# A two-layer decoder trunk: PSUM tiles of two banks, weight blocks split by alternate rows, and seven products in three column groups of a chunk's first block

## Chip, cores and metric

The kernel runs on one core of one Trainium2 chip. The metric is device time in microseconds (us) of one execution, lower is better. Three runs of the kernel before took 2023.47, 2025.87 and 2023.33 us, with a median of 2023.47.

## What is computed

The reference is a trunk of two layers over 256 tokens of width 2048, in float32. Layer 0 mixes by trailing means over windows of 2, 4, 8 and 16 tokens, layer 1 by causal dilated attention with 16 heads of 128; each mixer is followed by a layer norm with a scaled residual, a gated feed-forward block with a causal convolution of width 3, and another layer norm.

```python
# layer 0                                     # layer 1
mix = pool_mixer(h, w_in, w_grp, scale, w_out) # or dilated_attention(h, k, v, w_q, w_o)
h = layer_norm(ALPHA * h + mix, ln1_g, ln1_b)
u = h @ w_up                                   # 2048 -> 2 * 5504
c = conv_b + sum(conv_w[j] * shifted(u, j))    # width 3, causal
gate, val = split(c)
h = layer_norm(ALPHA * h + (silu(gate) * val) @ w_down, ln2_g, ln2_b)
```

Some 380 MB of weights are read once, and nearly all the arithmetic is matrix products of 256 tokens with those weights.

## The kernel before

**Products in two parts.** Each float32 operand is split into a high part, which the reduced float32 format of TensorE holds, and a low part, the rest. `do_split` (L74) makes the two parts of a weight block of 512 rows by 512 columns: ScalarE copies the high part `wh` (L82), VectorE subtracts to get the low part `wl` (L83). A product is then high times high, high times low and low times high.

**Units.** The work is a list `units`; each entry is one weight block, what TensorE does with it, and what follows once the group is closed (`post`). `run_units` (L126) goes through the list in order. Ahead of unit i it issues loads of up to 5 later units (three `raw` buffers, SyncE's queue) and splits of up to 3 later units (four buffers of `wh` and `wl`). Then TensorE's instructions of the unit are issued, then whatever `later(n, fn)` put off until now, then the unit's `post`. All engines work in this program order.

**Two kinds of group.** `group` (L177) with `mm_quad` (L150) makes features by tokens: four PSUM banks (`acc`, one per 128 output features), filled over several units, with one matmul of 512 columns (`wh` on both parts of the activations, L165) and one of 256 (`wl` on the high part, L166) for each 128 by 128 block. The last unit of a group goes bank by bank, the others row block by row block. `group_tm` (L189) makes tokens by features for the down projection and for V: banks `t0`, `t1`, and a unit either takes the plain way, 24 matmuls of 512 columns (`go_t`, L232, L238 to L240), or the way of seven products.

**Seven products.** For a block listed in `sevens`, the 512 by 512 weight block and the activations are cut in two by two parts, and seven products of sums of parts replace eight. Sums of weights are made by `split_sums` (L90) in two units, "a" and "b", out of one raw block; sums of activations by `left_sums` (L623), which takes the fourth of them, `own`, either at once or, through `own_at`, later with `last` (L661), where the plain way still needs the place in the tile `g` that it is written to. The unit pair has 42 matmuls of 256 columns (L227 to L229) into four banks, `t0`, `t1`, `s2`, `s3`. `early_post` (L822) folds the two `s` banks into the token tile `ht`, by accumulating DMAs on GpSimd's queue or by VectorE; `tm_post` (L844) adds the `t` banks.

**Feed-forward order.** Blocks of 512 hidden features are called q = 0 to 10. The down projection is made in chunks of blocks: 0 to 2, 3 to 5, 6 and 7, 8 to 10. Within a chunk there are four column groups c = 0 to 3 of 512 output columns. `weave` (L713) puts the units of chunk 0 and chunk 1 between units of the next up projections: four up units and three down blocks to one c. Blocks q = 0 and q = 3, the first of their chunks, take seven products in c = 2 and c = 3 only; the others of these chunks take them in every c.

**PSUM.** The pool `psp` holds eight tiles of one bank, handed out in program order (`bank`). Evacuation goes bank by bank: ScalarE copies one half, VectorE adds the other (L577 and L578 for up projections, L1020 and L1021 for Q and K, L473 and L475 for the mixer), or VectorE adds both halves onto the residual (L320 and L322 in `resid_last`, L313).

**Layer norm at the end of a layer.** `add_last` (L458) runs four groups c = 0 to 3 of the last projection onto the residual H[0] to H[3]. After c = 0, `shift` (L362) takes an estimate `cs` of the token means; it is subtracted from H[0] by VectorE (L372). For layer 0's feed-forward block, where `shifted` is set, it is taken off the other three by TensorE: a matmul with a matrix `neg1` into each of 12 banks (L172). `stats` squares and folds each H[q] into running sums `S` and `Q` (L345 to L350); `xp` makes scaled copies for the next projection (L395). One unit after the last group, `chain` (L400) has TensorE sum `S` and `Q` over the partitions (L401, L402), and the normalised tiles follow.

**Attention.** `scores` (L1034) makes the scores of two heads, each in a bank of its own, with softmax by VectorE and ScalarE head by head; `blocks` transposes, DMAs move 32 by 32 blocks, and `outputs` (L1085) multiplies by V, copies the high part (L1095) and subtracts the low part (L1096) head by head, for the output projection.

Of the kernel before, what the change touches and what calls it, by code (L numbers as in the profile page):

```python
# [32 lines left out]
def trunk(ctx: ExitStack, tc: tile.TileContext, x, pool_w_in, pool_w_grp, pool_scale, pool_w_out,  # L33
# [54 lines left out]
    B1, B2, N1, N2 = slice(0, 2), slice(2, 4), slice(0, 256), slice(256, 512)  # L88

    def split_sums(i, kind):  # L90
# [16 lines left out]
        V.tensor_tensor(r22, r22, r12, OP.subtract)  # L107
        both = r[:, :, N1].rearrange("p (b k) n -> p b k n", b=2)
        V.tensor_tensor(both, both, r22.unsqueeze(1).to_broadcast([P, 2, 2, 256]), OP.subtract)  # L109
# [40 lines left out]
    def mm_quad(xq, ps, first, last, mode, mid, shifted):  # L150
        def go(h, l):
# [4 lines left out]
            if first:  # L156
                for m in range(nb):
                    ps.append(bank("acc"))
            q = xq()
            n = XW if mode == "x" else T  # L160
            for i, (k, m) in enumerate(order):
                c = slice(m * P, (m + 1) * P)
                st, sp = first and k == 0, last and k == nk - 1
                if mode == "ab":
                    PE.matmul(ps[m], h[:, k, c], q[:, k, :, :T], start=st, stop=False)  # L165
                    PE.matmul(ps[m][:, :T], l[:, k, c], q[:, k, 0, :T], start=False, stop=sp and not shifted)  # L166
                else:
                    PE.matmul(ps[m][:, :n], h[:, k, c], q[:, k, 0, :n], start=st, stop=False)  # L168
                    PE.matmul(ps[m][:, :n], h[:, k, c], q[:, k, 1, :n], start=False, stop=False)  # L169
                    PE.matmul(ps[m][:, :n], l[:, k, c], q[:, k, 0, :n], start=False, stop=sp and not shifted)  # L170
                if sp and shifted:
                    PE.matmul(ps[m][:, :T], neg1, ST["cs"], start=False, stop=True)  # L172
# [4 lines left out]
    def group(w, r0s, c0, ncol, xqs, post, mode="ab", mids=(), shifted=False):  # L177
        ps = []
        for j, (r0, nr) in enumerate(r0s):
            last = j == len(r0s) - 1  # L180
            units.append((w[r0:r0 + nr, c0:c0 + ncol],
                          mm_quad(xqs[j], ps, j == 0, last, mode, mids[j] if j < len(mids) else None, shifted),
# [6 lines left out]
    def group_tm(w, r0s, c0, ncol, xqs, post, apart=False, seven=(), early=None):  # L189
# [5 lines left out]
        def opened():  # L195
            ps.extend([bank("t0"), bank("t1")])
            if seven:
                ps.extend([bank("s2"), bank("s3")])
# [3 lines left out]
        def mk_seven(kind, j):  # L202
            fst, fin, op, cl = j == 0, j == len(r0s) - 1, j == opening, j == closing

            def go(h, l):
# [4 lines left out]
                def a(k, t):  # L210
                    return lambda hl, kk: x[:, k + kk, hl, t * P:t * P + P]
# [5 lines left out]
                if kind == "a":  # L217
                    prods = [(a(0, 0), 0, N1, 2, 0, op, False), (a(2, 0), 2, N1, 0, 0, fst, False),
                             (sm(3), 2, N2, 0, 1, False, fin)]
                else:  # L220
                    prods = [(sm(0), 0, N2, 3, 1, op, False), (sm(1), 2, N2, 2, 1, False, cl),
                             (a(2, 1), 2, N1, 1, 0, fst, fin), (sm(2), 0, N1, 3, 0, False, cl)]
                for left, k0, n, b, half, opens, ends in prods:
                    to = ps[b][:, 256 * half:256 * half + 256]
                    for kk in range(2):
                        xh, xl, k = left(0, kk), left(1, kk), k0 + kk
# [36 lines left out]
        def done():  # L263
            if not apart:
# [3 lines left out]
                else:  # L268
                    post(1, ps[1], 0)
# [3 lines left out]
        for j, (r0, nr) in enumerate(r0s):  # L273
# [6 lines left out]
            units.append((src, mk(j), done if j == len(r0s) - 1 else None))  # L280

# [18 lines left out]
    neg1 = const.tile([P, P], F32R, name="neg1")  # L300
# [12 lines left out]
    def resid_last(c, first, lay, which, after):  # L313
        def post(ps):
            for m in range(4):
                y = H[c][:, m, :]
                if first and c == 0:
                    V.scalar_tensor_tensor(y, y, ALPHA, ps[m][:, :T], op0=OP.mult, op1=OP.add)
                else:
                    V.tensor_tensor(y, y, ps[m][:, :T], OP.add)  # L320
                if c < 3:
                    V.tensor_tensor(y, y, ps[m][:, T:], OP.add)  # L322
                if c == 3 and m % 2 == 1:
                    square(3, m - 1)
            if c == 0:
                s = fold(H[0], None, "S0", F32R)
# [16 lines left out]
    def fold(src, acc, nm, dt=F32):  # L343
        t2 = lnp.tile([P, 2, T], F32, name="fold2", tag="fold2")
        V.tensor_tensor(t2, src[:, 0:2, :], src[:, 2:4, :], OP.add)  # L345
        t1 = lnp.tile([P, T], dt, name=nm, tag=nm if acc is None and dt == F32 else "f1")
# [15 lines left out]
    def shift(s, first, lay, which):  # L362
        ps = bank("shift")
        PE.matmul(ps[:, :T], ones4, s, start=True, stop=True)
        cs = lnp.tile([P, T], F32R, name="cs", tag="cs")
        A.copy(cs, ps[:, :T])
        ST["cs"] = cs
        cb = cs.bitcast(F32).unsqueeze(1).to_broadcast([P, 4, T])
# [16 lines left out]

        later(1, one)
        later(2, two)

# [11 lines left out]
    def chain(ps, lay, which, after):  # L400
# [4 lines left out]
        ST["rs"], ST["mr"] = rs, mr  # L405
# [35 lines left out]
    def norm_evac(ps, nb, dst):  # L441
        wgb = lnp.tile([P, 4, 2], F32, name="wgb", tag="wgb", bufs=2)
        for m in range(nb):
            A.copy(wgb[:, m, :], ps[m][:, T:XW])
        for m0 in range(0, nb, 2):
            ts = [(m, dst(m)) for m in range(m0, min(nb, m0 + 2))]
            for m, t in ts:
                V.tensor_tensor(t, ps[m][:, :T], ST["rs"], OP.mult)
            for m, t in ts:
# [8 lines left out]
    def add_last(w, rows, srcs, first, lay, which, after=None):  # L458
        for c in range(4):
            group(w, rows, 512 * c, 512, srcs, resid_last(c, first, lay, which, after),  # L460
                  mode="a" if c == 3 else "ab", shifted=c > 0 and not first)
# [5 lines left out]
    def pool_post(g):  # L467
        def post(ps):
# [3 lines left out]
            for m in range(4):  # L472
                A.copy(p[:, m, PADW:], ps[m][:, :T])  # L473
                if g < 3:
                    V.tensor_tensor(p[:, m, PADW:], p[:, m, PADW:], ps[m][:, T:], OP.add)  # L475
# [32 lines left out]
    def x_quad(q, halves=(0, 1)):  # L508
        xin = XIN
        if halves[0] == 0:  # L510
            H[q] = hp.tile([P, 4, T], F32, name="h", tag="h")
            XC[q] = quad_tile("xc")
# [743 lines left out]
```

## Time and profile before

| | |
|---|---|
| runs, median (lowest to highest) | 2023.47 us (2023.33 to 2025.87) |
| profiled execution: its own time | 2024.13 us |
| its span, first to last instruction | 2022.0 us, at a granted TensorE clock of 1.000 |
| busy: TensorE, VectorE, ScalarE, GpSimd | 2014.2, 1719.5, 1270.1, 111.3 us |
| HBM read | 380.01 MB |

Times of single instructions are in us from the start of the span, "mean ns" is the duration of one, and "idle before" is how long the engine stood still before such an instruction and for whom. Ends of matmuls are modelled and overlap with the next one, so what a matmul takes from TensorE's time is read from one start to the next start.

### The profile page before, as it was taken

Reading aid. Unit: us, or ns where it says so; the run is one execution under the profiler, and the core shown is the slowest. Engines: PE = TensorE matmul, PEld = TensorE weight load, DVE = VectorE, ACT = ScalarE, POOL = GpSimd, SP = SyncE. Lnnn points to the kernel's source line nnn. Section 1 sums busy time; section 2 is a strip of 40 time slices with the busy share of each in tenths; the row PEclk is TensorE's granted clock in tenths of the full one; section 3 lists DMA queues with packets and bytes.
Section 4 is the critical chain, followed back from the end, with each engine's and each line's share of the span. In section 5 each row is a group of like instructions: output and inputs, shape, how many; then the busy total and the mean of one; then the engine's idle time right before and its main releaser. Section 6 shows DMA issues by size and latency. Waiting matters only on the chain.

```text
span 2022.0 us, 31645 instructions
## 1 busy us (share of the span) xinstructions
PE 2014.2 (100%) x12610; PEld 1809.2 (89%) x12610; DVE 1719.5 (85%) x2075; ACT 1270.1 (63%) x1708; POOL 111.3 (6%) x175
## 2 busy tenths in 40 slices
PE   9999999999999999999999999999999999999999
PEld 8898988899889988889898988998899989989987
DVE  6859887899789999889887878787889888989898
ACT  6544686667766686656544544487666676667672
POOL 2000000000000001100001021000001000100100
PEclk9999999999999999999999999999999999999999
DMA  8665477666666758875555656557666756666765
GB/s 259 208 205 187 164 208 211 189 190 224 215 184 192 239 178 228 219 228 179 178 194 174 214 166 205 182 187 215 184 208 190 225 186 219 198 213 194 210 214 181
DMA packets 273699, 406.73 MB, mean 201 GB/s; under 512 B 74782, under 2 KB 91060, under 8 KB 273296
## 3 DMA queue, kind: packets, MB, share of 16 engines
q1 hardware_dynamic: 259488, 388.93, 59.5%
q0 software_dynamic: 13632, 15.13, 5.0%
q8 instruction: 99, 1.62, 0.3%
q10 hardware_dynamic: 432, 0.66, 0.1%
q14 instruction: 48, 0.39, 0.1%
HBM read 380.01 MB, written 2.10 MB: 189 GB/s over the span
## 4 chain that ended last, share of the span: by engine, by line
PE 99%; DMA 0%; SPq 0%; DVE 0%; ACT 0%; issue 0%; DVEq 0%
PE acc L165 44%; PE acc L166 22%; PE s L228 3%; PE s L227 3%; PE s L229 3%; PE acc L169 3%; PE acc L170 3%; PE acc L168 3%; PE t L238 3%; PE t L240 3%; PE t L239 3%; PE t L228 2%; PE t L227 2%; PE t L229 2%; PE s L1040 0%; PE o L1093 0%
## 5 line engine op out<-in xcount | busy, mean ns | idle before, releaser
L165 PE MATMUL acc<-xc,wh 128*128 128x512 f32 x3264 | 1152.0, 396 | 0.0
L166 PE MATMUL acc<-xc,wl 128*128 128x256 f32 x3264 | 916.9, 281 | 0.0
L83 DVE TENSOR_TENSOR wl<-raw,wh 128x2048 fp32r<-128x2048 f32 (+2 forms) x313 | 676.0, 2165 | 207.8 <-ACT wh L82 206.4
L165 PEld LDWEIGHTS acc<-xc,wh 128*128 128x128 f32 x3264 | 616.2, 189 | 143.5 <-issue 0.3
L82 ACT CAST wh<-raw 128x2048 fp32r<-128x2048 f32 (+2 forms) x313 | 564.8, 1810 | 201.7 <-PE acc L165 92.2
L166 PEld LDWEIGHTS acc<-xc,wl 128*128 128x128 f32 x3264 | 615.5, 189 | 0.8 <-DVE wl L83 0.3
L96 ACT CAST wh<-raw 128x1024 fp32r<-128x1024 f32 x126 | 131.7, 1053 | 170.9 <-DVE raw L107 135.5
L97 DVE TENSOR_TENSOR wl<-raw,wh 128x1024 fp32r<-128x1024 f32 x126 | 150.4, 1221 | 3.5 <-ACT wh L96 3.5
L103 ACT CAST wh<-raw 128x1024 fp32r<-128x1024 f32 x126 | 98.7, 834 | 47.8 <-PE acc L165 24.6
L106 DVE TENSOR_TENSOR wl<-raw,wh 128x1024 fp32r<-128x1024 f32 x126 | 114.7, 951 | 4.2 <-ACT wh L103 4.0
L586 ACT ACTIVATE c<-u,cv 128x256 f32<-128x256 f32 x172 | 89.6, 593 | 19.6 <-DVE f L649 8.1
L271 POOL DMA_DIRECT2D ht<-w x24 | 20.4, 850 | 1435.3 <-DVE ht L853 388.1
L228 PE MATMUL t<-wl,g 128*128 128x256 f32 x328 | 92.3, 281 | 0.0
L227 PE MATMUL t<-wh,g 128*128 128x256 f32 x328 | 92.1, 281 | 0.0
L229 PE MATMUL t<-wh,g 128*128 128x256 f32 x328 | 91.9, 280 | 0.0
L577 ACT COPY u<-acc 128x256 f32<-128x256 f32 x164 | 53.8, 372 | 45.9 <-PE acc L166 45.9
L229 PE MATMUL s<-wh,xs 128*128 128x256 f32 x296 | 82.6, 279 | 0.0
L227 PE MATMUL s<-wh,xs 128*128 128x256 f32 x296 | 82.6, 279 | 0.0
L228 PE MATMUL s<-wl,xs 128*128 128x256 f32 x296 | 82.6, 279 | 0.0
L591 ACT ACTIVATE a<-u,cv 128x256 f32<-128x256 f32 x172 | 73.5, 499 | 12.3 <-DVE g L659 6.5
L109 DVE TENSOR_TENSOR raw<-raw 128x1024 f32<-128x1024 f32 x63 | 77.2, 1225 | 2.1
L591 ACT ACTIVATE u<-u,cv 128x256 f32<-128x256 f32 x172 | 73.5, 500 | 0.0
(337 smaller groups left out, 3540.3 us busy)
## 6 DMA issues: line engine op xcount, KB each, us to landing
raw<-in_ffn_w_up_dram SPq DMA_DIRECT2D x160, 1024.0 KB, 5.1
raw<-in_ffn_w_down_dram SPq DMA_DIRECT2D x80, 1024.0 KB, 5.2
raw<-in_pool_w_out_dram SPq DMA_DIRECT2D x16, 1024.0 KB, 5.0
raw<-in_shared_w_k_dram SPq DMA_DIRECT2D x16, 1024.0 KB, 5.3
raw<-in_attn_w_q_dram SPq DMA_DIRECT2D x16, 1024.0 KB, 5.4
raw<-in_shared_w_v_dram SPq DMA_DIRECT2D x16, 1024.0 KB, 5.3
raw<-in_attn_w_o_dram SPq DMA_DIRECT2D x16, 1024.0 KB, 5.3
raw<-in_pool_w_in_dram SPq DMA_DIRECT2D x12, 1024.0 KB, 5.6
```

The lines of the kernel that those rows point to most:

```text
L82: A.copy(wh[i][:, s], r[:, s])
L83: V.tensor_tensor(wl[i][:, s], r[:, s], wh[i][:, s].bitcast(F32), OP.subtract)
L96: A.copy(h[:, :, n], r[:, :, n])
L97: V.tensor_tensor(l[:, :, n], r[:, :, n], h[:, :, n].bitcast(F32), OP.subtract)
L103: A.copy(h[:, k, n], r[:, k, n])
L106: V.tensor_tensor(l[:, k, n], r[:, k, n], h[:, k, n].bitcast(F32), OP.subtract)
L165: PE.matmul(ps[m], h[:, k, c], q[:, k, :, :T], start=st, stop=False)
L166: PE.matmul(ps[m][:, :T], l[:, k, c], q[:, k, 0, :T], start=False, stop=sp and not shifted)
L227: PE.matmul(to, xh, h[:, k, n], start=opens and kk == 0, stop=False)
L228: PE.matmul(to, xh, l[:, k, n], start=False, stop=False)
L229: PE.matmul(to, xl, h[:, k, n], start=False, stop=ends and kk == 1)
L591: A.activation(to[:, m, :], u[:, m, i:i + T], AF.Copy, scale=cv[:, i, j:j + 1])
```

## The change

- PSUM becomes four tiles of two banks (`pair`). A single bank asked for takes a whole pair. Evacuations in `evac`, `pool_post`, `resid_last`, `norm_evac`, `qk_post` and `outputs`, and the softmax's first steps in `scores`, take both banks of a pair in one instruction.
- The weight block of the seven products is cut by alternate 128-row blocks (0 and 2 against 1 and 3), so that the three parts kept as they are form one run of 768 elements twice: one copy and one subtraction where there were two of each.
- `sevens[0]` and `sevens[3]` become (1, 2, 3): one more block of seven products in chunk 0 and one in chunk 1, in each of the two layers. `own` is made one column group earlier.
- The matmuls with `neg1` go; VectorE subtracts `cs` from H[1], H[2] and H[3], one instruction each, put off by 2, 3 and 4 units after `shift`.
- Small tiles (`fold2`, `f1`, `cs`) are replaced by one tile `w4` of four rows of 256. `early_post` makes its last two sums with one instruction and sends two DMAs of 256 KB where there were one of 256 KB and two of 128 KB.

```diff
-    psp = ctx.enter_context(tc.tile_pool(name="psp", bufs=8, space=bass.MemoryType.PSUM))
+    psp = ctx.enter_context(tc.tile_pool(name="psp", bufs=4, space=bass.MemoryType.PSUM))
+    def pair(nm):
+        return psp.tile([P, 2, 512], F32, name=nm, tag="ps")
     def bank(nm):
-        return psp.tile([P, 512], F32, name=nm, tag="ps")
+        return pair(nm)[:, 0, :]
...
-    B1, B2, N1, N2 = slice(0, 2), slice(2, 4), slice(0, 256), slice(256, 512)
+    B1, B2, N1, N2 = slice(0, 4, 2), slice(1, 4, 2), slice(256, 512), slice(0, 256)
...
-        parts = [(slice(0, 4), N1), (B2, N2)]
-        for k, n in parts:
-            A.copy(h[:, k, n], r[:, k, n])
+        hs, ls, rs = (t.rearrange("p (k b) n -> p k (b n)", b=2)[:, :, 256:] for t in (h, l, r))
+        A.copy(hs, rs)
         V.tensor_tensor(r12, r12, r11, OP.subtract)
-        for k, n in parts:
-            V.tensor_tensor(l[:, k, n], r[:, k, n], h[:, k, n].bitcast(F32), OP.subtract)
+        V.tensor_tensor(ls, rs, hs.bitcast(F32), OP.subtract)
...
-                if sp and shifted:
-                    PE.matmul(ps[m][:, :T], neg1, ST["cs"], start=False, stop=True)
...
     def resid_last(c, first, lay, which, after):
         def post(ps):
-            for m in range(4):
-                y = H[c][:, m, :]
+            for m, n, p in pairs(ps):
+                y = H[c][:, m:m + n, :]
...
-                    V.tensor_tensor(y, y, ps[m][:, :T], OP.add)
+                    V.tensor_tensor(y, y, p[:, :, :T], OP.add)
                 if c < 3:
-                    V.tensor_tensor(y, y, ps[m][:, T:], OP.add)
+                    V.tensor_tensor(y, y, p[:, :, T:], OP.add)
...
+        def less(q):
+            V.tensor_tensor(H[q], H[q], cb, OP.subtract)
         later(1, one)
         later(2, two)
+        if not first:
+            for q in (1, 2, 3):
+                later(1 + q, lambda q=q: less(q))
...
-        sevens[0] = sevens[3] = (2, 3)
+        sevens[0] = sevens[3] = (1, 2, 3)
...
-            for m in range(nb):
-                A.copy(u[:, m, 2:], ps[m][:, T:])
-                V.tensor_tensor(u[:, m, 2:], u[:, m, 2:], ps[m][:, :T], OP.add)
+            for m, n, p in pairs(ps, nb):
+                y = u[:, m:m + n, 2:]
+                A.copy(y, p[:, :n, T:])
+                V.tensor_tensor(y, y, p[:, :n, :T], OP.add)
...
-            own_at[chunks[n][0]] = ends[1][0]
+            own_at[chunks[n][0]] = ends[0][0]
...
+        both = pair("o")
         for m in ms:
             hd = slice(m * P, (m + 1) * P)
-            ps = bank("o")
+            ps = both[:, m % 2, :]
             t = pT.pop((hq, m))
             PE.matmul(ps[:, :T], vt[:, 0, hd], t[:, :T], start=True, stop=False)
             PE.matmul(ps[:, P:T], vt[:, 1, hd], t[:, T:], start=False, stop=True)
-            A.copy(oq[hq][:, m, 0, :T], ps[:, :T])
-            V.tensor_tensor(oq[hq][:, m, 1, :T], ps[:, :T], oq[hq][:, m, 0, :T].bitcast(F32), OP.subtract)
+        o = oq[hq][:, ms[0]:ms[0] + 2]
+        A.copy(o[:, :, 0, :T], both[:, :, :T])
+        V.tensor_tensor(o[:, :, 1, :T], both[:, :, :T], o[:, :, 0, :T].bitcast(F32), OP.subtract)
```

More of the change, by code (lines that the diff above doesn't have):

```diff
@@ L156, in go @@
             if first:
[L157 to L158 removed]
+                for m in range(0, nb, 2):
+                    ps.extend(two_banks("acc"))
             q = xq()
@@ L512, in x_quad @@
             XC[q] = quad_tile("xc")
+        if halves[0] == 0:
+            ST["xT"] = pair("xT")
         for half in halves:
-            ps = bank("xT")
+            ps = ST["xT"][:, half, :]
             for kk in range(2):
```

201 lines of the change are left out of this document (105 added, 96 removed).

## The prediction

> **What bounds the kernel now.** I read the page first: busy shares and the chain that ended last.
>
> ```profile
> span 2022.0 us, 31645 instructions
> PE 2014.2 (100%) x12610; PEld 1809.2 (89%) x12610; DVE 1719.5 (85%) x2075; ACT 1270.1 (63%) x1708; POOL 111.3 (6%) x175
> PE 99%; DMA 0%; SPq 0%; DVE 0%; ACT 0%; issue 0%; DVEq 0%
> ```
>
> The span is 2022.0 us and the execution's own time 2024.13, so 2.1 us lie around it. TensorE is busy for all but 8 us, and 99% of the chain are its matmuls. Since a busy TensorE may hide short waits, I read who waited for whom, and the clock:
>
> ```profile
> PE acc L168 <- ACT wh L82: 2.0, 1, 2.0
> PE warm L1139 <- DVE one L1135: 1.1, 1, 1.1
> PE xT L518 <- DMA xin<-in_x_dram: 0.5, 1, 0.5
> PE acc L170 <- DVE wl L83: 0.2, 1, 0.2
> core 0: 2022.0 us, clock 1.000
> ```
>
> These are all of TensorE's waits (total, times, longest): 3.8 us, all in the first microseconds, which the change leaves alone. So work taken from VectorE, ScalarE, GpSimd or the DMA queues gains nothing by itself; the time falls by what leaves TensorE's stream, and rises by every wait that the change puts there. VectorE, at 85%, is the engine that could cause one.
>
> **What leaves TensorE.** Starts in its timeline, where a plain block and then a block of seven products lie between up units:
>
> ```profile
> 402.38 0.39 PE L238 MATMUL t<-wh,g 128*128 128x512 f32 x1
> ...
> 407.96 0.40 PE L165 MATMUL acc<-xc,wh 128*128 128x512 f32 x1
> ...
> 413.62 0.28 PE L227 MATMUL s<-wh,g 128*128 128x256 f32 x1
> ...
> 418.50 0.40 PE L165 MATMUL acc<-xc,wh 128*128 128x512 f32 x1
> ```
>
> The plain block (24 matmuls of 512 columns) takes 407.96 - 402.38 = 5.58 us, the pair of seven products (42 of 256) 418.50 - 413.62 = 4.88. Each block that changes over saves 0.70. There are four: q = 0 and q = 3 in c = 1, in two layers. That is 2.8 us.
>
> The Trainium skill (TensorE: Matmul & The Clock Gate, Back-to-back issue gap) prices one warm matmul at N/2.4 + 2.5 ns; by that the block saves 24 x 215.8 - 42 x 109.2 = 593 ns, and the four 2.4 us, as an estimate. The rows decide: 2.8.
>
> The matmuls with `neg1`:
>
> ```profile
> L172 PE MATMUL acc<-cs,neg 128*128 128x256 f32 x12 | 3.4, 280 | 0.0
> 907.52 0.28 PE L172 MATMUL acc<-cs,neg 128*128 128x256 f32 x1
> 907.64 0.39 PE L165 MATMUL acc<-g,wh 128*128 128x512 f32 x1
> ```
>
> From start to start one takes 0.12 us, so twelve give 1.4 us. All other matmuls stay. TensorE loses 2.8 + 1.4 = 4.2 us, which is as much as the change can bring.
>
> **What VectorE gets and loses.** The prices:
>
> ```profile
> L83 DVE TENSOR_TENSOR wl<-raw,wh 128x2048 fp32r<-128x2048 f32 x273 | 623.9, 2288 | 194.3 <-ACT wh L82 193.1 <-PE acc L165 0.6
> L97 DVE TENSOR_TENSOR wl<-raw,wh 128x1024 fp32r<-128x1024 f32 x126 | 150.4, 1221 | 3.5 <-ACT wh L96 3.5
> L109 DVE TENSOR_TENSOR raw<-raw 128x1024 f32<-128x1024 f32 x63 | 77.2, 1225 | 2.1
> L107 DVE TENSOR_TENSOR raw<-raw 128x512 f32<-128x512 f32 x63 | 43.6, 692 | 2.2
> L83 DVE TENSOR_TENSOR wl<-raw,wh 128x1536 fp32r<-128x1536 f32 x24 | 42.1, 1754 | 11.4 <-ACT wh L82 11.2
> L320 DVE TENSOR_TENSOR h<-h,acc 128x256 f32<-128x256 f32 x40 | 16.0, 414 | 1.1 <-PE acc L170 1.1
> L955 DVE TENSOR_TENSOR vt<-vt,t 128x512 f32<-128x512 f32 x6 | 3.8, 679 | 0.0
> L372 DVE TENSOR_TENSOR h<-h,cs 128x1024 f32<-128x1024 f32 x3 | 3.7, 1219 | 0.0
> L521 ACT CAST xc<-xT 128x512 fp32r<-128x512 f32 x8 | 4.4, 589 | 9.4 <-PE xT L518 9.4
> ```
>
> A plain block costs VectorE one subtraction, 2.29 us. Seven products, with the merged subtraction of 1536 elements, cost 2 x 0.69 + 1.75 + 1.23 + 2 x 1.22 = 6.8 (sums of 512 elements twice, of 1024 once, low parts of 1024 twice), so 4.5 us more at each of the four sites. Merging two bank reads of 256 into one of 512 saves 2 x 0.41 - 0.68 = 0.15 each, the merged softmax, splits and `early_post` a little more; all of it lies beside TensorE and counts as zero, except where VectorE is last. ScalarE, at 63%, likewise. That an instruction reads two banks at one price is not in this trace; the bounds are 0.68 (same size, one bank) and 0.82 (two instructions), and I take the first, as the cost goes by elements.
>
> *The four sites.* In the 44 us where c = 1 gives way to c = 2:
>
> ```profile
> 402.00:446.00 44.00, 44.00 (x287) 39.93 (x286) 39.82 (x46) 26.34 (x35) 2.56 (x3) 1.00 0.64 186
> 441.83 2.28 DVE L83 TENSOR_TENSOR wl<-raw,wh 128x2048 fp32r<-128x2048 f32 x1
> 445.50 0.28 PE L166 MATMUL acc<-xc,wl 128*128 128x256 f32 x1
> ```
>
> VectorE is busy for 39.8 (39.82, the fourth column after the window), so 4.2 are free. The narrowest point there is this split: ready at 444.11, used at 445.50, 1.4 us in hand. The added 4.5, and TensorE 0.7 earlier, together 5.2, meet 4.2 of idle time and some 1 us of merged instructions. I take no wait. Without that cover it would be up to 5.2 - 1.4 = 3.8 us a site.
>
> *Two banks freed together.* A pair comes free only with its later half. The tight case is a new up group at the turn of a column group, whose banks the last up group held:
>
> ```profile
> 463.45 1.07 DVE L578 TENSOR_TENSOR u<-u,acc 128x256 f32<-128x256 f32 x3
> ...
> 466.34 0.39 PE L165 MATMUL acc<-xc,wh 128*128 128x512 f32 x1
> ```
>
> All four were empty at 464.52, 1.8 us before the first new matmul; two merged adds end no later than four. I price pairing at zero; above zero it would be at most the length of such an evacuation, about 1.4 us, where VectorE is late.
>
> *The end of layer 0's feed-forward block.* Here VectorE gets three subtractions, `less`, of 1.22 us:
>
> ```profile
> 908.12 1.76 DVE L83 TENSOR_TENSOR wl<-raw,wh 128x1536 fp32r<-128x1536 f32 x1 [1.10 <-ACT wh L82]
> ...
> 912.83 0.41 DVE L320 TENSOR_TENSOR h<-h,acc 128x256 f32<-128x256 f32 x1
> ...
> 928.79 1.41 DVE L320 TENSOR_TENSOR h<-h,acc 128x256 f32<-128x256 f32 x4
> ...
> 931.42 0.43 DVE L350 TENSOR_TENSOR S<-S 128x256 f32<-128x256 f32 x1
> ...
> 932.94 0.43 DVE L350 TENSOR_TENSOR Q<-Q 128x256 f32<-128x256 f32 x1
> 933.00 0.60 PE L401 MATMUL acc<-S,onesd 128*128 128x256 f32 x2
> 933.43 0.68 PE L402 MATMUL acc<-Q,onesd 128*128 128x256 f32 x2
> ```
>
> Between 908.12 and the last sum into `Q` VectorE is never idle, and TensorE takes `Q` at 933.43, when it has been ready (933.37) for 0.06 us: VectorE is as late as TensorE already. Behind `less` stand the folds of H[1], H[2] and H[3], and `chain` waits for them. Added: 3 x 1.22 = 3.7. Taken up: the 1.1 idle at 908, and what merged adds save. Four adds in a row take 1.41, 0.35 each, since neighbours overlap, and their sums onto the same tile somewhat more; so I count 0.1 for a pair merged, 0.4 each for c = 1 and c = 2 (eight into four) and 0.2 for c = 3. That is 2.1 in all, and `Q` comes about 1.5 us later (bounds: 0 if the queue finds more idle time, 2.6 if the adds save nothing). TensorE, without `neg1`, would be there 1.4 earlier. It pauses for 1.5 + 1.4 = 2.9 us in two pieces, ahead of `S` and ahead of `Q`. The 1.4 us gained turn into 1.5 lost.
>
> *The output projection.* The last two heads go to the block that starts just behind them:
>
> ```profile
> 1232.36 0.37 ACT L1095 CAST o<-o 128x256 fp32r<-128x256 f32 x1 [0.28 <-PE o L1094]
> 1232.76 0.43 DVE L1096 TENSOR_TENSOR o<-o 128x256 fp32r<-128x256 f32 x1 [0.23 <-ACT o L1095]
> 1232.86 0.40 PE L165 MATMUL acc<-o,wh 128*128 128x512 f32 x1
> ```
>
> The matmul at 1232.86 reads the third head of four, done before the copy at 1232.36. Merged, the copy starts there, takes 0.59, the subtraction 0.68: ready at 1233.65. A new wait of 0.8 us (bounds 0 and 0.9).
>
> **Sum.** -2.8 for seven products, +1.5 at `chain` in place of -1.4, +0.8 at the output projection: -0.5 us. The profiled 2024.13 becomes 2023.6; the median of the runs, 2023.47, is 0.7 below it, and becomes 2023.0.
>
> **Rivals.** *A, no pause at `chain` nor at the heads:* VectorE finds room. For it: small savings all along its queue. Against it: the unbroken queue from 908. Time 2023.47 - 4.2 = 2019.3, 0.21% faster.
>
> *B, VectorE falls behind at the four sites:* much of its 4.2 idle may be waits for ScalarE's copies that come again, and "a" and "b" count as two of the three units split ahead, so the look-ahead is shorter in time. If half of the uncovered 3.8 shows at each site, 4 x 1.9 = 7.6 are added: 2030.6, slower. It decides from 1.2 us a site. Against it: c = 2 and c = 3 have the same make-up already, and TensorE never waits in them.
>
> *C, the pause at `chain` costs clock:* after it TensorE would run its next unit at half rate. A unit there takes 5.75 us (927.25 to 933.00 by its starts), so +5.7: 2028.7. The trace speaks against it: the clock stays 1.000 with a wait of 2.0 us in the span.
>
> ```profile
> 927.25 0.28 PE L168 MATMUL acc<-xp,wh 128*128 128x258 f32 x1
> ```
>
> The rule behind it is the Trainium skill's (TensorE: Matmul & The Clock Gate, Part 1: The HAM clock gate): an idle window of about 3.4 us halves the clock. By that rule a pause of 2.9 us in two pieces keeps it, which agrees with the trace's wait of 2.0.
>
> *D, the change doesn't do what it says:* an instruction over two banks costs as much as two. Then `Q` comes 2.6 late instead of 1.5: 2024.1, no different.
>
> **Chances.** Forecast 0.62, A 0.20, B 0.12, C 0.03, D 0.03. A change of 0.2%, 4.0 us, is about what a measurement of this kernel can tell from none. A lies at that edge; I count 0.14 as faster. B and C give 0.15 slower. The rest, 0.71, is no difference. The forecast's own bounds are 2023.47 - 2.8 - 1.4 at the lowest and 2023.47 - 2.4 + 2.6 + 0.9 = 2024.6 at the highest; the range reaches down to A with a little spread, 2019.0, and up to 2026.0, past the highest of three runs before (2025.87), and leaves B and C out.
>
> **What would show it.** Right: 12,598 + 72 (four blocks, 42 for 24) matmuls in TensorE's row, that is 12,670; no L172; a wait of TensorE for `S` and `Q` of 2 to 3 us near 930; one of 0.8 for `o` near 1230; none for `wl` between 380 and 700 or 1470 and 1800; granted clock 1.000. Wrong: TensorE waiting for `wl` there (B), no wait at `Q` (A), or TensorE waiting for VectorE's evacuations at the start of a group, which would refute the price of pairing.

## The result and the profile after

The changed kernel takes 2030.49 us (median of 7 runs, 2028.32 to 2032.69) where the kernel before takes 2023.66 on the same chip (7 runs, 2023.33 to 2025.87): a ratio of 1.0028, 95% interval 1.0019 to 1.0037 (the ratio is an estimate of its own, not the quotient of the medians). It is slower by some 0.3%, and above the range that was forecast. The profiled execution after took 2029.47 us, 5.3 more than the one before.

The page of after first, with the shares of its chain of waits in the last row, then the view of waits, with all of TensorE's (us in total, times, longest; what was waited for stands behind the arrow):

```profile
span 2027.7 us, 31249 instructions
...
PE 2011.5 (99%) x12670; PEld 1808.6 (89%) x12670; DVE 1719.4 (85%) x1811; ACT 1260.8 (62%) x1538; POOL 90.5 (4%) x151
...
PE 93%; DVE 4%; DMA 1%; issue 1%; ACT 1%; SPq 0%; DVEq 0%; ACTq 0%
```
```profile
PE xT L544 <- DVE xc L548: 4.9, 4, 1.4
PE acc L183 <- ACT wh L99: 1.2, 1, 1.2
PE acc L425 <- DVE S L369: 1.2, 1, 1.2
PE t L253 <- DVE ht L880: 1.1, 1, 1.1
PE warm L1166 <- DVE one L1162: 1.1, 1, 1.1
PE acc L426 <- DVE Q L369: 0.8, 1, 0.8
PE acc L180 <- DVE o L1123: 0.7, 1, 0.7
PE acc L185 <- DVE wl L100: 0.2, 1, 0.2
```

Twelve neg1 matmuls left and 72 came, the 12,670 of the forecast, and TensorE is busy for 2.7 us less than before; the span is 5.7 longer, so TensorE stands idle more. Three of the waits were forecast (`S`, `Q`, `o`). Two were not: `xT` at the start and `t` at the end.

**Where the time went.** I follow one landmark after another through the two timelines, by its start:

| landmark | before | after | later by |
|---|---|---|---|
| transpose `vT`, behind the input's quarters | 40.67 | 45.06 | 4.4 |
| TensorE's first matmul on `Q`, layer 0's mixer | 223.04 | 227.43 | 4.4 |
| first scores of the attention | 985.27 | 989.38 | 4.1 |
| first matmul on `Q`, behind the attention | 1312.00 | 1316.76 | 4.8 |
| matmuls into `gb` with `dg`, the last of TensorE | 2015.10 | 2020.14 | 5.0 |
| end of the span | 2022.0 | 2027.7 | 5.7 |

So 4.4 of the 5.7 us are lost in the first 45. Here is the second quarter of the input in after's timeline (start, duration, engine, line; in brackets the idle time before it and what ended it):

```profile
11.64 0.93 PE L544 MATMUL xT<-ident,xin 128*128 128x128 f32 x4
...
12.61 0.59 ACT L547 CAST xc<-xT 128x512 fp32r<-128x512 f32 x1 [1.68 <-PE xT L544]
...
13.23 0.69 DVE L548 TENSOR_TENSOR xc<-xT,xc 128x512 fp32r<-128x512 f32 x1 [1.57 <-ACT xc L547]
...
13.97 0.66 PE L544 MATMUL xT<-ident,xin 128*128 128x128 f32 x4 [1.40 <-DVE xc L548]
...
22.16 0.66 PE L544 MATMUL xT<-ident,xin 128*128 128x128 f32 x4 [1.40 <-DVE xc L548]
...
30.36 0.66 PE L544 MATMUL xT<-ident,xin 128*128 128x128 f32 x4 [1.40 <-DVE xc L548]
```

Four transposes fill the first bank of the pair `xT`; ScalarE's copy and VectorE's subtraction read it; only when VectorE is done (13.92) does TensorE write the second bank, which nobody reads at that time. It waits 1.40 us each in the second, third and fourth quarter.

The same at the end, in the last group of tokens by features, which is filled bank by bank:

```profile
2008.10 0.39 PE L255 MATMUL t<-wh,g 128*128 128x512 f32 x1
...
2008.88 0.68 DVE L880 TENSOR_TENSOR ht<-ht,t 128x512 f32<-128x512 f32 x1
...
2009.62 0.39 PE L253 MATMUL t<-wh,g 128*128 128x256 f32 x1 [1.14 <-DVE ht L880]
```

`t1` is begun when VectorE has read `t0` (2009.56). And the other way round in the last microseconds, before and then after:

```profile
2015.10 2.84 PE L927 MATMUL gb<-g,dg 128*128 128x512 f32 x6
...
2016.41 1.46 DVE L932 SCALAR_TENSOR_TENSOR ht<-ht,mv,gb 128x512 f32<-128x512 f32 x2
```
```profile
2020.14 2.84 PE L952 MATMUL gb<-g,dg 128*128 128x512 f32 x6
...
2022.16 1.40 DVE L957 SCALAR_TENSOR_TENSOR ht<-ht,mv,gb 128x512 f32<-128x512 f32 x2 [0.63 <-PE gb L952]
```

Before, VectorE reads the first bank of `gb` 1.31 us after TensorE's start, while the later banks are being written; after, 2.02 us after it, when the second bank of the pair is complete too: 0.7 us, the last step of the table (5.0 to 5.7).

The middle went much as forecast. This is `chain`, then the last two heads:

```profile
936.00 0.70 PE L425 MATMUL acc<-S,onesd 128*128 128x256 f32 x2 [1.19 <-DVE S L369]
...
937.52 0.70 PE L426 MATMUL acc<-Q,onesd 128*128 128x256 f32 x2 [0.82 <-DVE Q L369]
...
1237.66 0.49 PE L180 MATMUL acc<-o,wh 128*128 128x512 f32 x1 [0.71 <-DVE o L1123]
```

One more wait stands only in the row of a weight load (PEld), not in the view of TensorE's waits above:

```profile
1539.07 0.19 PEld L181 LDWEIGHTS acc<-xc,wl 128*128 128x128 f32 x1 [0.42 <-DVE wl L100]
```

It is at one of the four sites, at the split that the prediction took as the narrowest point there, one layer later. TensorE loses 0.4 us by it (from 4.05 to 4.45 later than before). With it the table closes to 0.1 us: +4.4 at the start, -1.4 for two blocks and +1.1 at `chain` up to the scores, +0.7 at the heads, then -1.4 for two blocks, +0.4 here and +1.3 at `t`, and +0.7 at `gb`.

### The profile page after: what moved, and what is told of

Read it like the earlier page. It is cut to its first block, busy times and chain, and to the rows that moved or that the text cites. A ratio compares the mean times of both kernels' runs of the same rounds, so it can differ in the third digit from the quotient of the medians.

```text
span 2027.7 us, 31249 instructions
## 1 busy us (share of the span) xinstructions
PE 2011.5 (99%) x12670; PEld 1808.6 (89%) x12670; DVE 1719.4 (85%) x1811; ACT 1260.8 (62%) x1538; POOL 90.5 (4%) x151
## 4 chain that ended last, share of the span: by engine, by line
PE 93%; DVE 4%; DMA 1%; issue 1%; ACT 1%; SPq 0%; DVEq 0%; ACTq 0%
PE acc L180 42%; PE acc L181 21%; PE s L244 3%; PE s L242 3%; PE s L243 3%; PE acc L184 3%; PE acc L183 3%; PE acc L185 3%; PE t L244 2%; PE t L242 2%; PE t L243 2%; PE t L253 2%; PE t L254 2%; PE t L255 2%; DVE wl L100 1%
## 5 line engine op out<-in xcount | busy, mean ns | idle before, releaser
L100 DVE TENSOR_TENSOR wl<-raw,wh 128x2048 fp32r<-128x2048 f32 (+2 forms) x309 | 666.5, 2164 | 187.3 <-ACT wh L99 186.0
L99 ACT CAST wh<-raw 128x2048 fp32r<-128x2048 f32 (+2 forms) x309 | 556.1, 1806 | 176.2 <-PE acc L180 78.1
L113 ACT CAST wh<-raw 128x1024 fp32r<-128x1024 f32 x134 | 140.1, 1053 | 196.0 <-DVE raw L122 168.8
L114 DVE TENSOR_TENSOR wl<-raw,wh 128x1024 fp32r<-128x1024 f32 x134 | 159.9, 1222 | 2.0 <-ACT wh L113 2.0
L121 DVE TENSOR_TENSOR wl<-raw,wh 128x1536 fp32r<-128x1536 f32 x67 | 117.5, 1754 | 10.0 <-ACT wh L119 9.2
L119 ACT CAST wh<-raw 128x1536 fp32r<-128x1536 f32 x67 | 98.9, 1477 | 27.2 <-PE acc L180 15.0
L286 POOL DMA_DIRECT2D ht<-w x48 | 41.3, 1014 | 1449.1 <-DVE ht L878 582.4
L244 PE MATMUL t<-wh,g 128*128 128x256 f32 x352 | 98.9, 281 | 0.0
L242 PE MATMUL t<-wh,g 128*128 128x256 f32 x352 | 98.9, 281 | 0.0
L244 PE MATMUL s<-wh,xs 128*128 128x256 f32 x320 | 89.5, 280 | 0.0
L242 PE MATMUL s<-wh,xs 128*128 128x256 f32 x320 | 89.3, 279 | 0.0
L604 ACT COPY u<-acc 128x512 f32<-128x512 f32 x84 | 46.6, 572 | 42.8 <-PE acc L181 42.5
```

The lines of the kernel that those rows point to most:

```text
L99: A.copy(wh[i][:, s], r[:, s])
L100: V.tensor_tensor(wl[i][:, s], r[:, s], wh[i][:, s].bitcast(F32), OP.subtract)
L113: A.copy(h[:, :, n], r[:, :, n])
L114: V.tensor_tensor(l[:, :, n], r[:, :, n], h[:, :, n].bitcast(F32), OP.subtract)
L119: A.copy(hs, rs)
L121: V.tensor_tensor(ls, rs, hs.bitcast(F32), OP.subtract)
```

## The experiments

Each is after with the edit that is shown. Ratios are to the kernel before, measured on the same chip in the same hours, and carry a 95% interval. e1, e2, e3 and e6 ran together, e4, e7, e8 and e9, then e11, e12 and e13, and e14 by itself, so medians are compared within such a set.

| run | median, us | ratio | profiled, us |
|---|---|---|---|
| after | 2030.49 | 1.0028 (1.0019 to 1.0037) | 2029.47 |
| e1_x_first | 2027.53 | 1.0018 (1.0009 to 1.0027) | 2027.76 |
| e2_t_apart | 2028.32 | 1.0020 (1.0011 to 1.0029) | 2028.79 |
| e3_neg1 | 2027.00 | 1.0020 (1.0011 to 1.0029) | 2027.22 |
| e6_less_pool | 2034.21 | 1.0052 (1.0040 to 1.0065) | 2034.21 |
| e8_x_tiles | 2031.52 | 1.0032 (1.0020 to 1.0045) | 2031.53 |
| e4_three | 2023.19 | 0.9994 (0.9985 to 1.0003) | 2022.96 |
| e7_two_groups | 2032.55 | 1.0041 (1.0027 to 1.0055) | 2032.39 |
| e9_all | 2024.42 | 1.0000 (0.9991 to 1.0008) | 2023.27 |
| e11_o_banks | 2025.69 | 1.0006 (0.9997 to 1.0015) | 2025.57 |
| e12_x_banks | 2022.78 | 0.9994 (0.9985 to 1.0003) | 2024.11 |
| e13_pairs_only | 2028.08 | 1.0021 (1.0012 to 1.0030) | 2029.34 |
| e14_best | 2021.29 | 0.9988 (0.9979 to 0.9998) | 2020.91 |

### The start: order or tile

**e1_x_first**: all eight transposes of a quarter first, then the copies and subtractions.

```diff
                     PE.transpose(ps[:, kk * T + t * P:kk * T + t * P + P], xin[q, t][:, k * P:(k + 1) * P], ident)
+        for half in halves:
+            ps = ST["xT"][:, half, :]
             pv2 = ps.rearrange("p (k t) -> p k t", k=2)
```

> The changed kernel with one reordering in x_quad: all eight transposes of an input quarter are issued first, into both banks of the pair, and only then the two copies and two subtractions. Theory 'one tile' (a write to one bank of a pair waits for the reads of its other bank that were issued before it): TensorE's 4.9 us of waits for the subtractions of xc (3 of about 1.4, and smaller ones) go, and the run is 4.4 us shorter than the changed kernel, about 2025 in a profiled execution. Rival 'four slots' (the waits come because the pool has only four tiles to give): the order inside a tile changes nothing, the 4.9 us stay, 2029.5. Rival 'clock' (the pauses at the start also cost granted clock, as 0.997 to 0.999 in some executions of the changed kernel suggest): more than 4.4 us shorter, 5 to 7, and a granted clock of 1.000 in every execution.

The waits for `xc` fell from 4.9 to 0.5 us, and `vT` starts at 42.37, 2.7 earlier than after and 1.7 later than before. Part of the rest is three waits for `wl`, 0.9 us together, since VectorE now has both subtractions of a quarter to do at one time. The rival 'four slots' falls, since the order inside a tile did change the waits. The profiled execution is only 1.7 us shorter than after, not the 4.4 of the theory: 1.7 are left at the start, and the granted clock halved behind `chain` (below), which cost 1.2.

**e8_x_tiles**: the order of after, but each half in a tile of its own.

```diff
-        if halves[0] == 0:
-            ST["xT"] = pair("xT")
         for half in halves:
-            ps = ST["xT"][:, half, :]
+            ps = bank("xT")
...
-            before.setdefault(min(q + 1, 3), []).append(lambda s=s, pv2=pv2: A.copy(H[q][:, s, :], pv2))
+            A.copy(H[q][:, s, :], pv2)
```

> The input's transposes: each half gets a tile of one bank of its own instead of one bank of a tile of two; the order of the instructions stays that of after, but the copy of H is made at once, as in before. Theory one (a write into one bank waits for the reads of the other bank of the same tile): TensorE's 4.9 us of waits for xc, in four pieces, go although nothing is reordered, vT comes near 41 us instead of 45.06, and the time falls by some 4 us, to 2026 to 2027. Rival (the wait comes from the order of the instructions, copy and subtraction of the first half ahead of the transposes of the second): the waits stay, vT near 45, and the time stays near 2030.

The expectation is wrong in one thing: before puts the copy of H off, too. Here it had to come earlier, since a single bank takes a whole pair and there are four. The first rows are the second quarter, the others all of TensorE's waits that concern the start:

```profile
11.80 1.04 PE L542 MATMUL xT<-ident,xin 128*128 128x128 f32 x8
...
12.43 0.58 ACT L545 CAST xc<-xT 128x512 fp32r<-128x512 f32 x1 [2.05 <-PE xT L542]
```
```profile
PE acc L183 <- ACT wh L99: 3.9, 4, 1.1
...
PE acc L185 <- DVE wl L100: 0.9, 4, 0.2
...
PE xT L542 <- DMA xin<-in_x_dram: 0.5, 1, 0.5
```

All eight transposes run in one go with the order unchanged, and no wait for `xc` is left: it was the shared tile. The time gained nothing: the copies of H, now ahead of the copies of the weights on ScalarE, made TensorE wait 3.9 us for `wh` (1.2 in after), and in this execution the granted clock was 0.64 from 8 to 12 us. The mechanism is settled, its price is not, by this run alone.

**e12_x_banks** mends that: own tiles, and H copied half a unit earlier than in before. It has also what e11_o_banks has (below).

```diff
+            ps = bank("xT")
...
-            before.setdefault(min(q + 1, 3), []).append(lambda s=s, pv2=pv2: A.copy(H[q][:, s, :], pv2))
+            before.setdefault(q, []).append(lambda s=s, pv2=pv2: A.copy(H[q][:, s, :], pv2))
```

> As the one with heads in tiles of their own, but the transposes of the input in their old order, each half in a tile of its own, and the copy of H made half a unit earlier than in before (the slots are then free for the next quarter), not at once. If the own tile alone frees TensorE (as the vanished waits for xc say) and the copies at once were what cost 3.9 us of waits for wh, there is neither a wait for xc nor one for wh of 1 us in each quarter, vT comes at 40.7 to 41.5 us instead of 42.0, and the time is 0.5 to 1.3 us below that with all transposes first: about 2021. Rival (the copies of H collide with ScalarE's copies of the weights wherever they stand): waits for wh, vT at 43 or later, 2023 or more.

Neither wait is left from the second quarter on, and `vT` starts at 41.56, just above the forecast, with a lower clock from 8 to 16 us in this execution (0.87 and 0.71 in two stretches of 4 us). In e14_best, which has the same start at full clock, it starts at 39.84. The time missed the forecast of 2021 because of the heads.

### The end, and the end of layer 0

**e2_t_apart**: the second bank of the last group in a tile of its own.

```diff
-            ps.extend([t[:, 0, :], t[:, 1, :]])
+            ps.extend([t[:, 0, :], bank("t1") if apart else t[:, 1, :]])
```

> The changed kernel, in which the very last token group takes a tile of its own for each of its two token halves (t0 and t1) instead of the two banks of one pair. Theory 'one tile': TensorE's wait of 1.1 us (1.3 by its starts) near 2009 for VectorE's read of the first half goes, and the run is 1.3 us shorter, about 2028.2 profiled. Rival 'VectorE is late there' (the read itself comes late, and whatever TensorE does next waits for it): a wait of the same size moves to the next matmul that needs a bank, no change.

The wait of 1.1 us is gone; from the last matmul into `t0` to the first into `t1` it takes 0.22 us (2008.81 to 2009.03) instead of 1.52. The rival falls: no wait of that size came up elsewhere. The profiled execution is 0.7 us shorter, not 1.3, since its clock halved behind `chain` (below).

**e3_neg1**: the matmuls with `neg1` back, no `less`.

```diff
+                if sp and shifted:
+                    PE.matmul(ps[m][:, :T], neg1, ST["cs"], start=False, stop=True)
...
-        if not first:
-            for q in (1, 2, 3):
-                later(1 + q, lambda q=q: less(q))
```

> The changed kernel with the estimate of the means taken off H[1] to H[3] by the twelve matmuls with neg1 again, and without the three subtractions less on VectorE. Theory 'queue' (the three subtractions make VectorE's sums S and Q late): the waits of 1.2 us for S and 0.8 us for Q near 936 go, TensorE gets 1.4 us of matmuls back, and from the block before to the block after the chain it is 1.1 us shorter than the changed kernel: about 2028.4 profiled. Rival 'merged adds' (the adds over two banks come later than four single ones and delay the folds): the waits stay, and the run is 1.4 us longer.

The waits for `S` and `Q` are gone, although TensorE has its twelve matmuls back, and the `Q` behind the attention starts at 1315.06 where after has 1316.76. Of these 1.7 us, 0.2 come from the start (`vT` at 44.85): the edit is worth 1.5. At `chain` itself it is 1.1: from the first matmul of the unit before it to the first of the unit behind it TensorE takes 8.99 us in after (928.88 to 937.87), 6.47 in e3_neg1 (930.01 to 936.48) and 6.52 in before (927.25 to 933.77); that is 2.5 us of pauses in after, less the 1.4 of the matmuls. Another 0.3 lie between 950 and 966, where nothing was edited. The rival 'merged adds' falls.

**e6_less_pool**: the three subtractions on GpSimd.

```diff
-            V.tensor_tensor(H[q], H[q], cb, OP.subtract)
+            nc.gpsimd.tensor_tensor(H[q], H[q], cb, OP.subtract)
```

> The changed kernel with the three subtractions less on GpSimd instead of VectorE. Theory 'queue': VectorE's queue is 3.6 us shorter between 903 and 937, S and Q come in time or nearly so, and of the 2.0 us of waits at most 0.7 is left; 1.5 to 2.3 us shorter than the changed kernel, about 2027.5 profiled. Rival 'GpSimd is slow': each subtraction of 1024 elements takes several us there, H[1] to H[3] come late to the folds, and the wait for S and Q grows beyond 2 us; up to some us longer. Rival 'merged adds': waits as in the changed kernel, 2029.5.

```profile
L405 POOL TENSOR_TENSOR h<-h,fold 128x1024 f32<-128x1024 f32 x3 | 9.4, 3164 | 46.3 <-DVE h L339 46.3
```
```profile
PE acc L425 <- DVE S L369: 4.2, 1, 4.2
```

They take 3.16 us apiece against VectorE's 1.22, and the wait for `S` grew from 1.2 to 4.2 us. But no fold waits for GpSimd here. What came later is VectorE's own work beside GpSimd's (903.36 to 912.78), the four `xp` instructions, first in after, then in this run:

```profile
905.66 1.67 DVE L419 SCALAR_TENSOR_TENSOR xp<-h,vec,xp 128x256 fp32r<-128x256 f32 x4
```
```profile
905.34 8.13 DVE L419 SCALAR_TENSOR_TENSOR xp<-h,vec,xp 128x256 fp32r<-128x256 f32 x4
```

Three of them take 2.6 us each in place of 0.48, and each ends 0.3 us after one of GpSimd's three subtractions does. So the edit took 3.7 us of subtractions out of VectorE's queue and brought 6.5 us into it: the time of the rival 'GpSimd is slow' came about, by another way than its own. From `Q` of the mixer to the first scores the run takes 5.4 us longer than after: 3.0 of the wait, and the rest where the clock is halved (next).

**The clock behind `chain`.** These are stretches of 4 us (busy us of five engines, then the granted clock) of after, of e2_t_apart and of e6_less_pool:

```profile
934.00:938.00 4.00, 1.99 (x12) 1.36 (x11) 3.83 (x9) 4.00 (x8) 0.00 (x0) 1.00 0.76 262
938.00:942.00 4.00, 4.00 (x35) 3.97 (x34) 3.59 (x5) 2.40 (x4) 0.00 (x0) 1.00 0.01 4
```
```profile
934.00:938.00 4.00, 2.00 (x11) 1.34 (x10) 3.83 (x9) 4.00 (x8) 0.00 (x0) 0.96 0.76 262
938.00:942.00 4.00, 4.00 (x23) 3.91 (x23) 3.47 (x5) 2.51 (x5) 0.00 (x0) 0.61 0.02 4
```
```profile
938.00:942.00 4.00, 2.44 (x8) 1.85 (x9) 3.90 (x10) 3.66 (x8) 0.00 (x0) 0.69 0.58 225
942.00:946.00 4.00, 4.00 (x20) 4.00 (x20) 3.43 (x3) 2.84 (x3) 0.00 (x0) 0.50 0.18 27
```

After and e2_t_apart have the same instructions here and the same pause, but in the one execution the clock stays whole and in the other it halves: 23 matmuls in the second stretch instead of 35. From `Q` of the mixer to the first scores e2_t_apart takes 763.1 us (227.32 to 990.46), after 761.95 (227.43 to 989.38): 1.2 us. e1_x_first, with the same pause at 933, loses as much (clock 0.69 and 0.89 behind it). In e3_neg1, without the pause, the clock is 1.00 in all these stretches.

### Do they add up, and is anything else lost

**e4_three**: e1, e2 and e3 together.

> Three undos together: all transposes of a quarter of the input ahead of their reads, the last group's second bank in a tile of its own, and the neg1 matmuls back in place of the three subtractions less. The four blocks of seven products and all other pairs stay. If the three causes add up, by their sizes in the profiles one at a time (2.7 at the start, 1.1 at the end, 1.7 in the middle: 5.5 together), the profiled execution takes 2029.47 - 5.5 = 2024 and the median is 2023 to 2025, the same as before; nothing halves the clock behind the end of the first feed-forward block. Rival (what is lost lies in the pairs as such, spread over the kernel): at least 2027.

2022.96 profiled, 6.5 less than after where the sum said 5.5: 3.0 at the start, 1.5 up to the scores and 2.0 behind the attention (1.3 at `t`, and 0.4 since the wait for `wl` at 1539 is gone). The causes add up, and the rival, a loss spread over all pairs, falls. The kernel is level with before.

**e7_two_groups**: after with seven products as in before.

```diff
-        sevens[0] = sevens[3] = (1, 2, 3)
+        sevens[0] = sevens[3] = (2, 3)
...
-            own_at[chunks[n][0]] = ends[0][0]
+            own_at[chunks[n][0]] = ends[1][0]
```

> After, with first quarters of chunks back to seven products in two column groups of three (the first and last quarter), as in before; the pairs, less and the merged heads stay. By the prediction's first term (four blocks at 0.70 us) it takes 2.8 us more than after: 2033 where after has 2030.5. Rival (VectorE, with 4.5 us more work at each of these sites, already loses there what the blocks save): the same time as after, 2030, or less. The part of the change that this leaves should then be slower than before by some 9 us.

**e13_pairs_only**: the same edit on e11_o_banks.

> As the one with heads in tiles of their own, with first quarters of chunks back to seven products in two column groups: what is left of the change is the pairs, the alternate rows and the merged instructions, without the four places where pairs or subtractions made TensorE wait. If pairs cost nothing elsewhere, as the prediction has it, this takes the time of before, plus the 1.4 us by which the quarters of the input are later than in before: 0 to +1.5 us; and the four blocks of seven products are worth 2.8 us between this and the one with heads in tiles of their own. Rival (pairs cost a little in many places, which the blocks hide): 3 us or more above before.

From `vT` to the last matmuls with `dg` e7_two_groups takes 1977.6 us (45.12 to 2022.72) and after 1975.1 (45.06 to 2020.14), 2.5 more; e13_pairs_only 1975.9 (43.62 to 2019.56) and e11_o_banks 1973.2 (43.09 to 2016.24), 2.8 more. The four blocks bring 2.8, and 2.5 where what they add to VectorE's work delays a `wl`: after has the wait at 1539, the other three runs have none there. But e13_pairs_only came out 4.2 us above before by the medians, not 0 to 1.5. That is the number of the rival, but not its cause, since the loss has three places: the heads in single tiles, which it shares with e11_o_banks, cost 2.2 us (next), the start 2.9 instead of 1.4 (`vT` at 43.62), and the last reads of `gb` 0.7. These make 5.8 where the profiled spans differ by 5.1 (2027.1 and 2022.0); some 0.7 come back between `Q` of the mixer and the scores (761.75 us, before 762.23) and from `Q` behind the attention to `dg` (702.8, before 703.1).

### The heads

**e9_all**: e4_three with copy and subtraction per head, both heads still in one pair.

```diff
-        A.copy(o[:, :, 0, :T], both[:, :, :T])
-        V.tensor_tensor(o[:, :, 1, :T], both[:, :, :T], o[:, :, 0, :T].bitcast(F32), OP.subtract)
+        for i in range(2):
+            A.copy(o[:, i, 0, :T], both[:, i, :T])
+            V.tensor_tensor(o[:, i, 1, :T], both[:, i, :T], o[:, i, 0, :T].bitcast(F32), OP.subtract)
```

> As the three undos together, and the last two heads copied and split one by one again. The wait of 0.7 us for o goes, so 0.7 to 0.9 us less than with the three: 2022 to 2024. If the four blocks of seven products bring the 2.8 us that the prediction counts and nothing else is lost, it comes out below before by up to 2 us, about 0.1%, at the edge of what can be measured. Rival (the blocks bring less, or the pairs cost elsewhere): the same as before or above it.

```profile
1232.43 0.42 DVE L1132 TENSOR_TENSOR o<-o 128x256 fp32r<-128x256 f32 x1
...
1232.89 0.37 ACT L1131 CAST o<-o 128x256 fp32r<-128x256 f32 x1 [0.49 <-DVE o L1132]
...
1233.29 0.42 DVE L1132 TENSOR_TENSOR o<-o 128x256 fp32r<-128x256 f32 x1 [0.44 <-ACT o L1131]
```

ScalarE's copy of the second head waits for VectorE's subtraction of the first. TensorE's wait of 0.7 became three of 0.8 together: nothing gained, and the rival's forecast holds.

**e11_o_banks**: e4_three with each head in a tile of its own.

```diff
-        both = pair("o")
...
-            ps = both[:, m % 2, :]
+            ps = bank("o")
```

> The three undos together, and each of the last two heads written into a tile of its own, copied and split by itself, as in before. Theory (the extra wait comes from the shared tile: with one tile ScalarE's copy of the second head waited 0.49 us for VectorE's subtraction of the first): the wait of TensorE for o goes, 0.7 to 0.9 us less than the three undos alone: profiled 2022.1, ratio to before about 0.999. Rival (two instructions a head keep o late in any case, since VectorE reaches them later than in before): waits for o of 0.7 to 0.8 us remain, the same time as the three undos.

The wait for `o` at the output projection went, but TensorE now waits twice for a slot, 1.5 us together, since each head holds a whole pair:

```profile
1024.95 0.50 PE L255 MATMUL t<-wh,xc 128*128 128x512 f32 x1 [1.27 <-DVE o L1129]
```

From the first scores to the `Q` behind the attention it takes 328.9 us, e4_three 327.4, before 326.7. Both theories fall; the merged heads, 0.7 us over before, are the cheapest with pairs.

**e14_best**: e4_three with the start of e12_x_banks.

> The three undos with the input's transposes as in the run that gives each half a tile of its own and copies H half a unit earlier (vT came sooner there than with all transposes first), and the last two heads merged in one pair as in after (single tiles for them hold whole pairs, and the next group then waited 1.5 us for a slot). By the waits of those profiles, 1.5 us less than with heads in single tiles plus the 0.7 us wait for o: about 0.8 to 1.5 us below that run, 2021 to 2022, ratio to before 0.9985 to 0.9992, that is faster than both kernels by about 0.1%. Rival (each repair shifts a wait elsewhere, as the heads in single tiles did): the same as that run or above it.

```profile
PE warm L1170 <- DVE one L1166: 1.1, 1, 1.1
PE acc L180 <- DVE o L1127: 0.7, 1, 0.7
PE xT L548 <- DMA xin<-in_x_dram: 0.6, 1, 0.6
```

These are all its waits. At 2021.29 us it beats both kernels, before by 0.12% (0.02 to 0.21).

## Why the prediction was wrong

**The step that failed** is "I price pairing at zero". It was worked out from one question, when a pair comes free for the next group, and that answer held: e4_three leaves all such pairs in place and shows no wait at the start of a group. The question that was left out is what happens inside a pair while it is in use. With one tile over two banks a write into one bank waits for the reads of the other (`xT`, `t`), and a read of one for the writes of the other (`gb`). Three places fill and empty a pair bank by bank, and none was looked for. The bound that was given, at most 1.4 us "where VectorE is late", came from the same question. Measured were 4.4 us at the start, 1.3 at the end of the last group, 0.7 in the last reads, 6.4 in all (the one at `gb` was not undone by a run; it is read from the two traces). Without them the profiled 2029.47 would be 2023.1, and the forecast by its own sum was 2023.6; the other terms miss by less. The Trainium skill (PSUM — Partial Sum Buffer, PSUM bank collisions raise a hardware error) has PSUM guarded by semaphores by bank and group of partitions, or simply by bank; the waits here go by the tile, as e8_x_tiles and e2_t_apart show, so that a tile of two banks is guarded as one.

Point by point:

- Four blocks of seven products, -2.8: 2.8 between e13 and e11, 2.5 between e7 and after.
- `chain`, +1.5 net: 1.1. A pause of 2.9 us was forecast; by the starts it is 2.5, of which the view of waits shows 1.2 and 0.8. The mechanism is as forecast (e3), the size 0.4 too large.
- The output projection, +0.8: a wait of 0.71, and 0.7 between landmarks.
- The four sites, no wait for `wl`: one site of four has one, which costs 0.4 us, at the point that was called the narrowest. This is rival B's mechanism, but B needed 1.2 us a site and falls by its size. The 0.2 us for `wl` in the view of waits lie at the start, and before has them too. Rival A, no pause at `chain` nor at the heads, falls by the waits above.
- An instruction on two banks costs as one of its size (rival D falls): an evacuation of 512 elements over two banks takes VectorE 0.68 us, in before 512 in one bank took 0.679:

```profile
917.57 0.68 DVE L337 TENSOR_TENSOR h<-h,acc 128x512 f32<-128x512 f32 x1
```

- Rival C, that the pause costs clock, was put at 0.03, since "the clock stays 1.000 with a wait of 2.0 us in the span". That was one execution: of the 90 executions of before that ran beside the experiments, 24 have a granted clock of 0.999. Behind `chain` it does happen, in some executions, at 1.2 us and not at the 5.7 of a whole unit at half rate. That accounts for part of the gap between after's profiled execution, whose clock stayed at 1.000, and its median, 1.0 us above it: of the seven executions four have a granted clock of 0.997 to 0.999. How many of these lost it at `chain` and how many at the start, no row tells.

What the prediction named as a refutation, TensorE waiting for VectorE's evacuations, is what the profile showed, though inside a pair and not at the start of a group.

## What to carry to other kernels

Before two PSUM banks become one tile, ask of every place not only when the pair comes free, but whether one bank is written while the other is read, or whether two engines read the two at once (e9); there, keep tiles of one bank, or write both before the first read. A pool of pairs makes every single bank cost a pair, so a repair with single tiles is itself paid in slots. A view of waits can leave out what stands only in the weight loads, as at 1539.

## What the runs showed of the hardware

Two waits of TensorE of 2.0 us together (1.2 and 0.8), with a pair of short matmuls between, are enough to halve the granted clock, in some executions and not in others. In e2_t_apart (starts of every third matmul) it looks like this:

```profile
939.47 0.42 PE L183 MATMUL acc<-xp,wh 128*128 128x258 f32 x1
...
940.12 0.42 PE L183 MATMUL acc<-xp,wh 128*128 128x258 f32 x1
...
941.28 0.28 PE L183 MATMUL acc<-xp,wh 128*128 128x258 f32 x1
...
941.63 0.28 PE L183 MATMUL acc<-xp,wh 128*128 128x258 f32 x1
```

Three matmuls take 0.65 us, then 0.35. The records of the clock show what goes with it. In e1, e2 and e8 the clock is 0.50 for 3.41 us (935.49 to 938.90, 937.68 to 941.10, 939.32 to 942.73), and from there to its fall at the end of the span it is 1085.44 us in all three, 318 times 3.4133: the changes lie on a grid of such steps. Counted back from the fall at its end (2025.79), after has an edge of the grid at 936.94, between the two waits. These are the steps that hold the waits, with TensorE's busy time and the clock, in e2_t_apart (and the step behind), then in after:

```profile
934.27:937.68 3.41, 1.41 (x7) 0.80 (x6) 3.27 (x8) 3.41 (x8) 0.00 (x0) 1.00 0.87 299
937.68:941.10 3.42, 3.42 (x16) 3.28 (x16) 3.42 (x6) 2.33 (x3) 0.00 (x0) 0.50 0.02 5
```
```profile
933.52:936.94 3.42, 2.00 (x13) 1.39 (x12) 3.28 (x7) 3.14 (x8) 0.00 (x0) 1.00 0.80 271
936.94:940.35 3.41, 2.83 (x21) 2.77 (x22) 3.38 (x7) 3.08 (x3) 0.00 (x0) 1.00 0.17 64
```

In e1, e2 and e8 all 2.0 us of idle time fall into one step, and the clock is halved in the next; in after (1.4 and 0.6) and e7 (1.2 and 0.8) an edge divides them, and the clock stays. These are five executions as they fell, and no run moved the grid on purpose. The Trainium skill (TensorE: Matmul & The Clock Gate, Part 1: The HAM clock gate) ties the halving to an idle window of about 3.4 us; these runs show it after less idle time than that, 2.0 us of 3.41, and not in one piece.
